# Attention scores: two heads turned in one block, and a high-by-high product of 64 rows

## The chip, the cores and the metric

The kernel runs on one core of one Trainium2 chip. The metric is the device time of one execution in microseconds (us); three runs of the kernel before gave a median of 2147.78 us, from 2147.52 to 2148.46. Engines are called as in the profile: PE (TensorE, matrix products and transposes; PEld is its loading of the stationary operand), DVE (VectorE), ACT (ScalarE), POOL (GpSimd) and SP (which issues the transfers).

## The reference

A trunk of two layers over 1024 tokens of width 1024. The first layer mixes tokens by a causal convolution, the second by attention in a sliding window of 128 keys with 16 query heads, 4 key and value heads (4 query heads share one) and head width 64. Each layer ends with layer norms, a squared-ReLU MLP of width 4096 and a gated embedding. All is float32. What the change touches is the scores of the attention:

```python
k = partial_rope((x @ w_k).reshape(B, T, N_KV_HEADS, HEAD_DIM), cos, sin)
q = partial_rope((x @ w_q).reshape(B, T, N_HEADS, HEAD_DIM), cos, sin)
q = q.reshape(B, nb, BLOCK, N_KV_HEADS, Q_PER_KV, HEAD_DIM)
scores = jnp.einsum("bnqkgd,bnskd->bnkgqs", q, kk,
                    preferred_element_type=jnp.float32) * (1.0 / math.sqrt(HEAD_DIM))
...
lse = jnp.logaddexp(jax.nn.logsumexp(scores, axis=-1, keepdims=True), sink)
probs = jnp.exp(scores - lse).astype(vv.dtype)
out = jnp.einsum("bnkgqs,bnskd->bnqkgd", probs, vv)
```

`kk` holds for each block of 128 queries the keys of the block before and of the own block; the first block has the own keys alone.

## The kernel before

**Two parts for each number.** A product in float32r (PE's faster format) keeps fewer bits than float32. So each operand is split into a high part, rounded to float32r, and a low part, the rest. `split` (line 652) does this with one ACT copy (high) and one DVE subtraction (low). `mm3` (line 656) then sums three products, high by high, high by low and low by high, in one PSUM bank.

**An order written by a planner.** The program is first recorded, each operation with an engine, its tiles and an assumed duration (`cost`, line 281). `schedule` (line 311) then plays the record through with these durations, gives tiles their buffers as they come free, and takes on each engine what is ready, the earliest recorded first. The engines run the result in that fixed order, so operations of neighbouring blocks stand mixed on each engine. All are issued from line 459, so the profile shows the same line everywhere, and groups are told apart by their tiles. Buffers are named by tag: `g` and `t` are tiles of 128x512 in SBUF, `B` holds keys (and later the residual stream), `ps`, `tr`, `sc`, `pv` are PSUM banks. `SLOTS` (line 47) says how many buffers each tag has; `move` hands a buffer from one tag to another. In the attention two `ps` banks become `sc`, one becomes `pv`.

**Keys** (in `attention`, line 1616). The projected keys and values of 8 token tiles come in two groups (tiles 4 to 7, then 0 to 3). For each tile, `rope` (line 1600) leaves 128 tokens x 4 heads x 64 in `kf`. It is split into high and low, the two laid side by side for each head in `kt`, and four transposes turn `kt`, one key head each: rows 0 to 63 of the result are the high part of the head, rows 64 to 127 the low part. Four ACT copies put them into `kT[g, half]`. For tiles 3 and 4 one more copy goes to `k34`, since block 4 needs keys of both halves of the tokens side by side.

**Queries and scores.** For each of 2 pairs of key heads and each of 8 blocks, 512 columns of queries (8 heads) are projected, and `rope` puts them into `q1`. POOL copies each head twice, side by side, into two tiles `qf`, one for each key head. `scores` (line 1729) is called once for each key head and block, 32 times in all. It turns its four heads with four transposes, so that rows 0 to 63 and rows 64 to 127 of the result both hold the head, and splits the result into `qT[0]` (high) and `qT[1]` (low). Each head then has two products of 128 rows with the same keys: `qT[0]` by `kT`, which gives high by high and high by low, and `qT[1]` by `kT`, which gives low by high and low by low:

```python
nc.tensor.matmul(ps[:, j, 0 : nb * P], qT[0][:, qs], ks, start=True, stop=False)
nc.tensor.matmul(ps[:, j, 0 : nb * P], qT[1][:, qs], ks, start=False, stop=True)
```

The scores have 256 columns (two blocks of keys), 128 in block 0. The rest of `scores` selects by mask (ACT copy, DVE `copy_predicated`), takes the maximum (DVE), the exponential with its sum (ACT) and the division (POOL). `values` (line 1780) runs two calls later: it turns the probabilities, splits them and multiplies by the values.

**Around it.** Before the attention stand the gated embedding of layer one, after it `mix_out` (output projection and layer norm). Both are long rows of PE products of 512 columns. The products of the query projections stand between those of the scores on PE.

Of the kernel before, what the change touches and what calls it, by code (L numbers as in the profile page):

```python
# [10 lines left out]
F32 = mybir.dt.float32  # L11
F32R = mybir.dt.float32r
AF = mybir.ActivationFunctionType
ALU = mybir.AluOpType

P = 128
# [7 lines left out]
HD = 64  # L24
# [7 lines left out]
WSLOTS = 5  # L32
# [7 lines left out]
LO = 288  # L40
LAG = 5
SC = 144
WAIT = 250.0
MIX_GROUPS = (
    ((0, 1, 2, 3), (4, 5, 6, 7)), ((0, 1), (2, 3), (4, 5), (6, 7)),
)
SLOTS = dict(raw=2, wh=WSLOTS, wl=WSLOTS, zz=1, A=9, B=8, X=8, E=4, bo=2, g=4, z=4, t=5, v=1, sm=16,
             ps=6, tr=2, sc=0, pv=0, mid=0)


# [139 lines left out]
class Recorder:  # L190
# [120 lines left out]
    def schedule(self):  # L311
# [85 lines left out]
        while True:  # L397
# [21 lines left out]
            p, i, o = heapq.heappop(rdy[e])  # L419
            if WAIT and fut[e] and e != "tensor":  # L420
                r, p2, i2, o2 = fut[e][0]
# [70 lines left out]
class Emit:  # L492
# [1123 lines left out]
    def attention(self):  # L1616
        nc, d, ws = self.nc, self.d, self.ws
        ac = self.sb("cst", n=256 + NT * 32 + 2 * NH)
        nc.sync.dma_start(ac[:, 0 : 256 + NT * 32], d["aconst"])
        self.own, self.ownT = ac[:, 0:P], ac[:, P : 2 * P]  # L1620
        self.rt = ac[:, 256 : 256 + NT * 32].rearrange("p (t e) -> p t e", t=NT)
        o = 256 + NT * 32
        self.sink, self.nsink = ac[:, o : o + NH], ac[:, o + NH : o + 2 * NH]
        nc.sync.dma_start(self.sink, d["sinks"].to_broadcast([P, NH]))
        nc.vector.tensor_scalar(out=self.nsink, in0=self.sink, scalar1=-1.0, scalar2=None, op0=ALU.mult)
        nc.vector.tensor_scalar(out=self.sink, in0=self.sink, scalar1=HD ** 0.5, scalar2=None, op0=ALU.mult)

        kT = {(g, p): self.sb("B", F32R) for p in range(2) for g in range(4)}  # L1630
        k34 = nc.tile("mid", (P, 1024), F32R).rearrange("p (g b t) -> p g b t", g=4, b=2)
        vf = [self.sb("A") for j in range(4)]
        ws.add(*[d["w_kv"][u] for u in range(4)])
        us = ws.get(4)
        for gp in range(2):
            ws.add(*self.low["w_q"][4 * gp : 4 * gp + 4])
        ws.pump()
        nc.move("raw", "mid")
        for tg in (range(4, 8), range(0, 4)):
            nc.slack = WORK_SLACK  # L1640
            for k in range(4 if tg[0] else 0):
                self.work("w_o", k, "X")
            nc.slack = 0.0
            for ps, t in zip(self.tok_group(tg, us), tg):
                nc.scalar.copy(vf[t // 2][:, t % 2 * 256 : (t % 2 + 1) * 256], ps[:, 256:512])
                kf = self.sb("t")[:, 0:256]
                self.rope(ps[:, 0:256], kf, t, 4)
                kt = self.sb("t", F32R)
                kv = kt.rearrange("p (g r e) -> p g r e", g=4, r=2)
                self.split(kf.rearrange("p (g e) -> p g e", g=4), kv[:, :, 0, :], kv[:, :, 1, :])  # L1650
                pt = self.transpose4(self.blocks(kt.bitcast(F32)))
                for g in range(4):
                    nc.scalar.copy(kT[g, t // 4][:, t % 4 * P : (t % 4 + 1) * P], pt[:, g * P : (g + 1) * P])
                if t in (3, 4):
                    nc.scalar.copy(k34[:, :, t - 3, :], pt.rearrange("p (g t) -> p g t", g=4))
        ws.done(4)
        self.kT, self.k34 = kT, k34

        for a, b in (("ps", "sc"), ("ps", "sc"), ("ps", "pv"), ("bo", "v"), ("bo", "v"), ("z", "v")):
            nc.move(a, b)  # L1660
        att = [self.pair("XE"[t // 4], F32R) for t in range(NT)]
        pend = []
        for gp in range(2):
            us = ws.get(4)
            for n in range(NT):
                ps = self.tok_group([n], us)[0]

                q1 = self.sb("t")
                self.rope(ps, q1, n, 8)
                qf = [self.sb("t") for gl in range(2)]  # L1670
                for gl in range(2):
                    src = q1[:, gl * 256 : (gl + 1) * 256].rearrange("p (h e) -> p h e", e=HD)
                    nc.gpsimd.tensor_copy(
                        qf[gl].rearrange("p (h r e) -> p h r e", r=2, e=HD), src.unsqueeze(2).to_broadcast([P, 4, 2, HD])
                    )

                col = n % 2 * 256 + gp * P
                own = vf[n // 2][:, col : col + P].rearrange("p (g e) -> p g e", g=2)
                if n == 0:
                    vd = [self.value_forms(own, q1 if gp == 0 else None)]  # L1680
                else:
                    if n > 1:
                        vd = [self.value_forms(last, q1 if n < 3 and gp == 0 else None)]
                    df = self.sb("t")[:, 0:P].rearrange("p (g e) -> p g e", g=2)
                    nc.vector.tensor_tensor(out=df, in0=own, in1=last, op=ALU.subtract)
                    vd = [vd[0], self.value_forms(df, q1 if n < 3 and gp == 0 else None)]
                last = own
                for gl in range(2):
                    if gp == 0:
                        dst = [a.rearrange("p (k t) -> p k t", k=4)[:, 2 * gl : 2 * gl + 2, :] for a in att[n]]  # L1690
                    else:
                        dst = [x[:, 2 * gl : 2 * gl + 2, n % 4 * P : (n % 4 + 1) * P] for x in self.xT[1, n // 4]]
                    p = self.scores(n, 2 * gp + gl, qf[gl])
                    pend.append((p, gl, vd, dst))
                    if len(pend) > 2:
                        self.values(*pend.pop(0))
            ws.done(4)
        for p in pend:
            self.values(*p)
        nc.move("mid", "raw")  # L1700
        for a, b in (("ps", "sc"), ("ps", "sc"), ("ps", "pv"), ("bo", "v"), ("bo", "v"), ("z", "v")):
            nc.move(b, a)

        self.x = []
        for t in range(NT):
            xt = [self.sb("AB"[t // 4]) for q in range(2)]
            for q in range(2):
                nc.sync.dma_start(xt[q], self.xsp[t // 4][t % 4 * P : (t % 4 + 1) * P, q * HT : (q + 1) * HT])
            self.x.append(xt)
        self.hid_tags = ("X", "E")  # L1710
        gb = self.load_row("g", d["mix_g"][1:2]), self.load_row("g", d["mix_b"][1:2])

        def lhs(t, kb):
            if kb < 4:
                return [a[:, kb * P : (kb + 1) * P] for a in att[t]]
            return self.xs(kb, t * P, P)

        self.mix_out(1, self.low["w_o"] + [d["w_o"][1, u] for u in range(4)], gb, range(NT), lhs)
# [10 lines left out]
    def scores(self, n, g, qf):  # L1729

        nc = self.nc
        nb = min(n, 1) + 1
        hs = slice(4 * g, 4 * g + 4)
        pq = self.transpose4(self.blocks(qf))
        qT = [self.sb("g", F32R) for j in range(2)]
        self.split(pq, *qT)
        sm = self.small(16)
        mx, nm, su = (sm[:, 4 * i : 4 * i + 4] for i in range(3))
        if n == 4:
            ks = self.k34[:, g].rearrange("p b t -> p (b t)")  # L1740
        else:
            o = (n % 4 + 1 - nb) * P
            ks = self.kT[g, n // 4][:, o : o + nb * P]

        s = nc.tile("z", (P, 4 * SC)).rearrange("p (h s) -> p h s", h=4)
        with nc.after(qf) if n == 0 else contextlib.nullcontext():
# [3 lines left out]
        for jj in range(2):  # L1750
            ps = self.ps("sc").rearrange("p (a b) -> p a b", a=2)
            for j in range(2):
                qs = slice((2 * jj + j) * P, (2 * jj + j + 1) * P)
                nc.tensor.matmul(ps[:, j, 0 : nb * P], qT[0][:, qs], ks, start=True, stop=False)
                nc.tensor.matmul(ps[:, j, 0 : nb * P], qT[1][:, qs], ks, start=False, stop=True)
            dst = s[:, 2 * jj : 2 * jj + 2, 0:P]
            if n:
                nc.scalar.copy(dst, ps[:, :, 0:P])
            nc.vector.copy_predicated(
                out=dst, mask=self.own.bitcast(mybir.dt.int32).unsqueeze(1).to_broadcast([P, 2, P]),  # L1760
                data=ps[:, :, (nb - 1) * P : nb * P],
            )
        nc.vector.reduce_max(out=mx, in_=s[:, :, 0:P], axis=mybir.AxisListType.X)
        nc.vector.scalar_tensor_tensor(
            out=nm, in0=mx, scalar=-(HD ** -0.5), in1=self.nsink[:, hs], op0=ALU.mult, op1=ALU.min
# [7 lines left out]
        for h in range(4):  # L1773
            nc.gpsimd.tensor_scalar(
                out=s[:, h, 0:P], in0=s[:, h, 0:P], scalar1=su[:, h : h + 1], scalar2=0.0,
# [170 lines left out]
```

## Time and profile before

| what | value |
|---|---|
| median of three runs | 2147.78 us |
| the profiled execution, its own time | 2149.95 us |
| its span in the profile | 2148.2 us |
| queries, scores and values (first to last product of scores) | 1175.6 to 1350.6 us |
| keys and values projected and turned | 1135 to 1175.6 us |

A row of the profile's groups gives line, engine, operation, tiles (result <- sources, buffer numbers left out), shapes and count, then the busy time, the mean duration of one, and the time the engine idled before them. A matmul row ends with the columns of its result: 128x512 is a product of 512 columns, and 128*128 says that its stationary operand has 128 rows and 128 columns. A transpose is a matmul with the tile `ident` among its operands. Products overlap on PE: each has a duration of its own, and what it costs in a dense row is the distance from its start to the next start. A row of the timeline gives the start, the time up to the last end, and how many like instructions stand in it.

### The profile page before, as it was taken

Reading aid. Unit: us, or ns where it says so; the run is one execution under the profiler, and the core shown is the slowest. Engines: PE = TensorE matmul, PEld = TensorE weight load, DVE = VectorE, ACT = ScalarE, POOL = GpSimd, SP = SyncE. Lnnn points to the kernel's source line nnn. Section 1 sums busy time; section 2 is a strip of 40 time slices with the busy share of each in tenths; the row PEclk is TensorE's granted clock in tenths of the full one; section 3 lists DMA queues with packets and bytes.
Section 4 is the critical chain, followed back from the end, with each engine's and each line's share of the span. In section 5 each row is a group of like instructions: output and inputs, shape, how many; then the busy total and the mean of one; then the engine's idle time right before and its main releaser. Section 6 shows DMA issues by size and latency. Waiting matters only on the chain.

```text
span 2148.2 us, 29826 instructions
## 1 busy us (share of the span) xinstructions
PE 2130.2 (99%) x10084; PEld 1765.3 (82%) x10084; DVE 1756.9 (82%) x2821; ACT 1096.2 (51%) x2098; POOL 285.5 (13%) x510
## 2 busy tenths in 40 slices
PE   9999999999999999999999999999999999999999
PEld 7888888888888888888788878887888888888877
DVE  6667788999897788876984888689999888788688
ACT  5333353655554533335855888455455454333484
POOL 0000052200000000001320656240000000000042
PEclk9999999999999999999999999999999999999999
DMA  7443554878786755655487022765788785575726
GB/s 237 114 111 89 171 178 172 263 233 272 257 268 223 281 174 197 204 186 216 150 283 254 11 89 70 228 227 182 252 288 294 272 300 169 182 235 169 262 75 230
DMA packets 203113, 433.21 MB, mean 202 GB/s; under 512 B 22353, under 2 KB 50641, under 8 KB 202961
## 3 DMA queue, kind: packets, MB, share of 16 engines
q1 hardware_dynamic: 202960, 431.32, 60.8%
q8 instruction: 79, 1.29, 0.2%
q14 instruction: 74, 0.60, 0.1%
HBM read 286.79 MB, written 144.44 MB: 201 GB/s over the span
## 4 chain that ended last, share of the span: by engine, by line
PE 45%; ACT 2%; DVE 2%; DMA 2%; issue 1%; POOL 0%; POOLq 0%; ACTq 0%; DVEq 0%
PE ps L459 34%; PE tr L459 11%; ACT z L459 1%; DVE z L459 0%; DVE B L459 0%; DMA raw<-form 0%; DMA wl<-gate_low_t 0%; DMA xh<-in_w_gate_dram 0%; POOL sm L459 0%; ACT xh L459 0%; DMA raw<-gate_t 0%; ACT t L459 0%; DVE t L459 0%; DMA raw<-in_w_q_dram 0%; ACT wh L459 0%
## 5 line engine op out<-in xcount | busy, mean ns | idle before, releaser
L459 PE MATMUL ps<-xh 128*128 128x512 f32 x618 | 240.4, 389 | 0.0
L459 PE MATMUL ps<-xl,xh 128*128 128x512 f32 x618 | 240.4, 389 | 0.0
L459 PE MATMUL ps<-xh,xl 128*128 128x512 f32 x618 | 240.4, 389 | 0.0
L459 PE MATMUL ps<-xh,wh 128*128 128x512 f32 x588 | 229.3, 394 | 0.9 <-ACT xh L459 0.9
L459 PE MATMUL ps<-xl,wh 128*128 128x512 f32 x588 | 229.4, 391 | 0.2 <-DVE xl L459 0.2
L459 PE MATMUL ps<-xh,wl 128*128 128x512 f32 x588 | 228.8, 390 | 0.0
L459 ACT CAST wh<-raw 128x1024 fp32r<-128x1024 f32 (+2 forms) x156 | 145.6, 937 | 128.4 <-PE ps L459 72.0
L459 POOL TENSOR_SCALAR sm<-sm 128x1 f32<-128x1 f32 x72 | 26.6, 373 | 1366.2 <-DVE E L459 612.8
L459 PE MATMUL ps<-wh,xh 128*128 128x512 f32 (+1 forms) x492 | 195.6, 398 | 2.5 <-DVE t L459 1.5
L459 PE MATMUL ps<-wl,xh 128*128 128x512 f32 (+1 forms) x492 | 195.5, 397 | 0.6 <-DMA wl<-gate_low_t 0.6
L459 PE MATMUL ps<-wh,xl 128*128 128x512 f32 (+1 forms) x492 | 195.6, 398 | 0.0
L459 ACT CAST wh<-g 128x512 fp32r<-128x512 f32 x108 | 64.5, 620 | 153.6 <-PE ps L459 75.3
L459 ACT CAST xh<-wh 128x1024 fp32r<-128x1024 f32 x76 | 79.7, 1049 | 118.3 <-PE ps L459 90.9
L459 PEld LDWEIGHTS ps<-xh 128*128 128x128 f32 x618 | 116.0, 188 | 24.2
L459 PEld LDWEIGHTS ps<-xh,xl 128*128 128x128 f32 x618 | 116.0, 188 | 24.1
L459 PEld LDWEIGHTS ps<-xl,xh 128*128 128x128 f32 x618 | 116.0, 188 | 24.0
L459 PEld LDWEIGHTS ps<-xh,wh 128*128 128x128 f32 x588 | 110.8, 188 | 25.6 <-ACT xh L459 1.3
L459 PEld LDWEIGHTS ps<-xh,wl 128*128 128x128 f32 x588 | 110.4, 188 | 23.4
L459 PEld LDWEIGHTS ps<-xl,wh 128*128 128x128 f32 x588 | 110.7, 188 | 21.8 <-DVE xl L459 0.7
L459 DVE TENSOR_TENSOR wl<-raw,wh 128x1024 fp32r<-128x1024 f32 (+1 forms) x100 | 101.2, 1013 | 25.3 <-ACT wh L459 24.5
L459 DVE TENSOR_TENSOR E<-cst,g 128x1152 fp32r<-128x1152 f32 x64 | 86.1, 1353 | 43.1 <-PE ps L459 40.9
L459 DVE TENSOR_TENSOR xl<-wh,xh 128x1024 fp32r<-128x1024 f32 x76 | 92.8, 1221 | 29.1 <-ACT xh L459 29.1
(441 smaller groups left out, 5402.5 us busy)
## 6 DMA issues: line engine op xcount, KB each, us to landing
wh<-hid SPq DMA_DIRECT2D x78, 512.0 KB, 4.1
raw<-in_w_up_dram SPq DMA_DIRECT2D x61, 512.0 KB, 4.3
wl<-in_w_down_dram SPq DMA_DIRECT2D x58, 512.0 KB, 4.8
hid<-zz SPq DMA_DIRECT2D x96, 256.0 KB, 4.2
hid<-t SPq DMA_DIRECT2D x70, 256.0 KB, 2.9
raw<-hid SPq DMA_DIRECT2D x30, 512.0 KB, 3.8
scr<-zz SPq DMA_DIRECT2D x128, 64.0 KB, 2.1
B<-scr SPq DMA_DIRECT2D x32, 256.0 KB, 4.1
```

What stands on the lines that cost most here:

```text
L459: getattr(getattr(nc, o.eng), o.name)(*a, **k)
```

## The change

Keys: `kf`, not its split parts, is turned, two heads in one transpose, two transposes a tile. Head g then stands in rows 0 to 63 (even g) or 64 to 127 (odd g): its `own` rows. ACT copies the high part to new tiles `kH`; DVE subtracts it from PSUM into the own rows of `kT`, which so holds the low part there, and ACT copies the high part into the other rows. `kH` takes two buffers each from `g` and `t` until the last block.

Queries: the copies on POOL go. `scores` turns two heads in one transpose, two transposes a call. Head 2j+e of the call stands in rows e*64 and on, columns j*128 and on. The split takes two ACT copies and two DVE subtractions of 64x256, which put the high part into the own rows of one tile `qT` and the low part into the other rows. One product of 128 rows then gives high by low and low by high (crosswise), and one product of 64 rows, own rows alone, high by high. Low by low is no longer formed. Block 4, whose high keys stand in two tiles, has two products of 64 rows and 128 columns in place of one of 256. The heads of the two banks are numbered so that order and results stay the same.

The core of the diff:

```diff
+ROWS = slice(0, P // 2), slice(P // 2, P)
+KH_FROM = "ggtt"
...
+        kH = {(j, p): self.sb("kh", F32R) for p in range(2) for j in range(2)}
...
+        for a in KH_FROM:
+            nc.move(a, "kh")
...
-                kt = self.sb("t", F32R)
-                kv = kt.rearrange("p (g r e) -> p g r e", g=4, r=2)
-                self.split(kf.rearrange("p (g e) -> p g e", g=4), kv[:, :, 0, :], kv[:, :, 1, :])
-                pt = self.transpose4(self.blocks(kt.bitcast(F32)))
+                pt = self.transpose4([kf[:, j * P : (j + 1) * P] for j in range(2)])
+                cols = slice(t % 4 * P, (t % 4 + 1) * P)
+                for j in range(2):
+                    nc.scalar.copy(kH[j, t // 4][:, cols], pt[:, j * P : (j + 1) * P])
                 for g in range(4):
-                    nc.scalar.copy(kT[g, t // 4][:, t % 4 * P : (t % 4 + 1) * P], pt[:, g * P : (g + 1) * P])
-                if t in (3, 4):
-                    nc.scalar.copy(k34[:, :, t - 3, :], pt.rearrange("p (g t) -> p g t", g=4))
+                    own, other = ROWS[g % 2], ROWS[1 - g % 2]
+                    hi = kH[g // 2, t // 4][own, cols].bitcast(F32)
+                    dst = kT[g, t // 4]
+                    nc.vector.tensor_tensor(
+                        out=dst[own, cols], in0=pt[own, g // 2 * P : (g // 2 + 1) * P], in1=hi, op=ALU.subtract
+                    )
+                    nc.scalar.copy(dst[other, cols], hi)
+                    if t in (3, 4):
+                        nc.scalar.copy(k34[:, g, t - 3, :], dst[:, cols].bitcast(F32))
...
-                qf = [self.sb("t") for gl in range(2)]
-                for gl in range(2):
-                    src = q1[:, gl * 256 : (gl + 1) * 256].rearrange("p (h e) -> p h e", e=HD)
-                    nc.gpsimd.tensor_copy(
-                        qf[gl].rearrange("p (h r e) -> p h r e", r=2, e=HD), src.unsqueeze(2).to_broadcast([P, 4, 2, HD])
-                    )
...
+        for a in KH_FROM:
+            nc.move("kh", a)
...
-        pq = self.transpose4(self.blocks(qf))
-        qT = [self.sb("g", F32R) for j in range(2)]
-        self.split(pq, *qT)
+        pq = self.transpose4([qf[:, j * P : (j + 1) * P] for j in range(2)])
+        own, other = ROWS[g % 2], ROWS[1 - g % 2]
+        qT = self.sb("g", F32R)
+        src = [(qT[own, e * 256 : (e + 1) * 256], qT[other, e * 256 : (e + 1) * 256], pq[ROWS[e], 0:256]) for e in range(2)]
+        for hi, lo, ps in src:
+            nc.scalar.copy(hi, ps)
+        for hi, lo, ps in src:
+            nc.vector.tensor_tensor(out=lo, in0=ps, in1=hi.bitcast(F32), op=ALU.subtract)
...
         if n == 4:
             ks = self.k34[:, g].rearrange("p b t -> p (b t)")
+            kh = [(0, P, self.kH[g // 2, 0][own, 3 * P :]), (P, P, self.kH[g // 2, 1][own, 0:P])]
         else:
             o = (n % 4 + 1 - nb) * P
             ks = self.kT[g, n // 4][:, o : o + nb * P]
+            kh = [(0, nb * P, self.kH[g // 2, n // 4][own, o : o + nb * P])]
...
-                qs = slice((2 * jj + j) * P, (2 * jj + j + 1) * P)
-                nc.tensor.matmul(ps[:, j, 0 : nb * P], qT[0][:, qs], ks, start=True, stop=False)
-                nc.tensor.matmul(ps[:, j, 0 : nb * P], qT[1][:, qs], ks, start=False, stop=True)
+                qs = slice((jj + 2 * j) * P, (jj + 2 * j + 1) * P)
+                nc.tensor.matmul(ps[:, j, 0 : nb * P], qT[:, qs], ks, start=True, stop=False)
+                for o, w, k in kh:
+                    nc.tensor.matmul(ps[:, j, o : o + w], qT[own, qs], k, start=False, stop=o + w == nb * P)
```

More of the change, by code (lines that the diff above doesn't have):

```diff
@@ L46 @@
 )
-SLOTS = dict(raw=2, wh=WSLOTS, wl=WSLOTS, zz=1, A=9, B=8, X=8, E=4, bo=2, g=4, z=4, t=5, v=1, sm=16,
+SLOTS = dict(raw=2, wh=WSLOTS, wl=WSLOTS, zz=1, A=9, B=8, X=8, E=4, bo=2, g=4, z=4, t=5, v=1, kh=0, sm=16,
              ps=6, tr=2, sc=0, pv=0, mid=0)
@@ L1647, in attention @@
                 self.rope(ps[:, 0:256], kf, t, 4)
-                kt = self.sb("t", F32R)
-                kv = kt.rearrange("p (g r e) -> p g r e", g=4, r=2)
-                self.split(kf.rearrange("p (g e) -> p g e", g=4), kv[:, :, 0, :], kv[:, :, 1, :])
-                pt = self.transpose4(self.blocks(kt.bitcast(F32)))
+                pt = self.transpose4([kf[:, j * P : (j + 1) * P] for j in range(2)])
+                cols = slice(t % 4 * P, (t % 4 + 1) * P)
+                for j in range(2):
+                    nc.scalar.copy(kH[j, t // 4][:, cols], pt[:, j * P : (j + 1) * P])
                 for g in range(4):
-                    nc.scalar.copy(kT[g, t // 4][:, t % 4 * P : (t % 4 + 1) * P], pt[:, g * P : (g + 1) * P])
-                if t in (3, 4):
-                    nc.scalar.copy(k34[:, :, t - 3, :], pt.rearrange("p (g t) -> p g t", g=4))
+                    own, other = ROWS[g % 2], ROWS[1 - g % 2]
[7 more added lines that the diff above has]
+                        nc.scalar.copy(k34[:, g, t - 3, :], dst[:, cols].bitcast(F32))
         ws.done(4)
-        self.kT, self.k34 = kT, k34
+        self.kT, self.k34, self.kH = kT, k34, kH
         for a, b in (("ps", "sc"), ("ps", "sc"), ("ps", "pv"), ("bo", "v"), ("bo", "v"), ("z", "v")):
@@ L1692, in attention @@
                         dst = [x[:, 2 * gl : 2 * gl + 2, n % 4 * P : (n % 4 + 1) * P] for x in self.xT[1, n // 4]]
-                    p = self.scores(n, 2 * gp + gl, qf[gl])
+                    p = self.scores(n, 2 * gp + gl, q1[:, gl * 256 : (gl + 1) * 256])
                     pend.append((p, gl, vd, dst))
```

## The prediction

> **What bounds the kernel now.** I read the page first, then the busy time by stretches around the attention, then the groups by shape inside it, the waits of PE, and last the timeline of PE, where the cost of single products can be read.
>
> ```profile
> span 2148.2 us, 29826 instructions
> PE 2130.2 (99%) x10084; PEld 1765.3 (82%) x10084; DVE 1756.9 (82%) x2821; ACT 1096.2 (51%) x2098; POOL 285.5 (13%) x510
> PEclk9999999999999999999999999999999999999999
> PE 45%; ACT 2%; DVE 2%; DMA 2%; issue 1%; POOL 0%; POOLq 0%; ACTq 0%; DVEq 0%
> ```
>
> PE is busy for 99% of the span, at full granted clock in every slice, and leads the chain that ended last. A product taken away there should be time saved, as long as its place is dense. So I looked at the stretches that the change touches (keys; queries, scores and values; the output projection):
>
> ```profile
> core 0: us, PE busy (x) PEld busy (x) DVE busy (x) ACT busy (x) POOL busy (x), PEclk, DMA share, GB/s
> 1135.00:1175.60 40.60, 40.23 (x198) 33.23 (x197) 18.12 (x60) 26.98 (x81) 2.50 (x7) 1.00 0.81 277
> 1175.60:1350.60 175.00, 174.09 (x985) 143.59 (x984) 151.14 (x403) 147.90 (x493) 106.49 (x260) 1.00 0.20 64
> 1350.60:1400.00 49.40, 49.40 (x223) 40.22 (x222) 29.44 (x52) 18.69 (x44) 5.73 (x12) 1.00 0.72 233
> ```
>
> In the 175 us of the scores PE is busy for 174.1, but DVE has 151.1 (86%) and ACT 147.9 (85%) as well: the other engines have some 24 us of room, no more. The view of the waits names for PE from 1190 to 1352 us only two, of 0.3 and 0.2 us:
>
> ```profile
> PE ps L459 <- POOL z L459: 0.3, 1, 0.3
> PE tr L459 <- DVE t L459: 0.2, 1, 0.2
> ```
>
> Busy time hides short pauses, since products overlap, so the cost of one product has to be read from starts. The timeline of PE in the scores:
>
> ```profile
> 1202.00 0.40 PE L459 MATMUL ps<-wl,xh 128*128 128x512 f32 x1
> 1202.23 0.39 PE L459 MATMUL ps<-wh,xl 128*128 128x512 f32 x1
> 1202.46 0.60 PE L459 MATMUL ps<-ident,t 128*128 128x128 f32 x4
> ...
> 1222.78 0.64 PE L459 MATMUL ps<-raw,g 128*128 128x256 f32 x4
> 1223.26 0.39 PE L459 MATMUL ps<-wh,xl 128*128 128x512 f32 x1
> ...
> 1225.32 0.39 PE L459 MATMUL ps<-wh,xl 128*128 128x512 f32 x1
> 1225.78 0.47 PE L459 MATMUL ps<-A,v 128*128 128x512 f32 x1
> ```
>
> A product of 512 columns is followed by the next start after 0.23 us. Four products of 256 columns take 1223.26 - 1222.78 = 0.48 us from start to start, 0.120 each. Four transposes end 0.60 us after the first start; one lasts 0.272 us by its row below, so their starts are (0.60 - 0.272) / 3 = 0.109 us apart. The last two rows show a pause that no view calls idle: 0.46 us in place of 0.23.
>
> ```profile
> L459 PE MATMUL tr<-B,g x112: 221/282/389, 1175.8 to 1349.4; 128*128 128x256 f32 x96, 128*128 128x128 f32 x16
> L459 PE MATMUL ps<-ident,t x132: 270/272/276, 1139.7 to 1343.4; 128*128 128x128 f32 x132
> L459 PE MATMUL ps<-wh,xl x195: 388/393/481, 1135.2 to 1399.5; 128*128 128x512 f32 x195
> ```
>
> **The change, part by part.** *Transposes.* The 32 calls of `scores` have two fewer each, the 8 key tiles two fewer each: 64 + 16 = 80. At 0.109 us that is -8.7 us of PE in dense stretches.
>
> *Products of the scores.* Each head keeps two products, one now with 64 rows. Block 4 has three: 4 key heads x 4 heads = 16 products of 256 columns become 32 of 128 columns. At the cost of a transpose for 128 columns, 32 x 0.109 - 16 x 0.120 = +1.6 us. The balance of PE, if 64 rows cost what 128 do, is -7.1 us. It also counts as 80 - 16 = 64 fewer instructions, 10020 in place of 10084, which the program of the changed kernel has.
>
> *Products of 64 rows among those of 128.* Every product of the profile before is 128*128, so no row shows what a change of the row count costs. In the order that the planner writes for the changed kernel there are 144 products of 64 rows, mostly single (the crosswise product of a head, then its high-by-high product): PE goes from one row count to the other 252 times. Bounds: the end on the one side is nothing. Changes of another kind, from product to transpose and back, stand in the rows above at no cost (0.109 and 0.23 us are the same there as in rows of a kind), and this is the row that speaks for nothing. The end on the other side is the part of a product that the next one overlaps: a product of 256 columns lasts 0.282 us and the next starts after 0.120, so 0.162 us would be exposed if a product of another row count had to wait until the one ahead has left the array. It is the same 0.16 us for 512 columns (0.39 - 0.23) and for a transpose (0.272 - 0.109). That is 252 x 0.162 = 40.8 us. A change of kind keeps the 128x128 shape, so its rows do not settle what another row count does, and no pair of products in the trace differs in it. I can exclude neither end and take the middle, 0.08 us, an estimate from the two: +20.2 us. Break-even is at 7.1 / 252 = 0.028 us, so five sixths of the way between the ends lie on the slower side.
>
> The Trainium skill speaks against the change here: in its page TensorEngine Tiling (Array Packing), section Key Properties, "Mode switching requires drain". It gives no price; by it the case of no cost would be out, and nothing in this case's trace can yet show whether that is so.
>
> Could products of 64 rows be cheaper than those of 128? The distances above go with columns (0.23, 0.120, 0.109), and at 128 columns something other than columns holds them. Loading is the candidate:
>
> ```profile
> L459 PEld LDWEIGHTS tr<-B,g 128*128 128x128 f32 x96 | 15.1, 189 | 4.5 <-ACT g L459 1.7 <-DVE g L459 0.8 <-DVE z L459 0.5
> L459 PEld LDWEIGHTS ps<-ident,t 128*128 128x128 f32 x96 | 12.1, 140 | 2.9
> ```
>
> A shorter load (140 against 189 ns) does not make transposes closer than 0.109 us, so I expect no gain from fewer rows; the end of the range for it is 96 products of 256 columns at 0.109 in place of 0.120, about -1 us.
>
> *The split.* DVE, ACT and POOL rows of the scores:
>
> ```profile
> L459 DVE TENSOR_TENSOR g<-ps,g 128x512 fp32r<-128x512 f32 x27 | 18.5, 690 | 4.0 <-ACT g L459 3.7
> L459 DVE TENSOR_TENSOR t<-t,ps 64x256 f32<-64x256 f32 x58 | 24.6, 424 | 6.6 <-ACT t L459 4.4
> L459 ACT CAST g<-ps 128x512 fp32r<-128x512 f32 x27 | 15.6, 581 | 1.0 <-PE ps L459 0.7
> L459 ACT COPY t<-ps 64x256 f32<-64x256 f32 x58 | 21.0, 362 | 6.7 <-PE ps L459 3.9 <-DVE t L459 2.1
> L459 POOL COPY t<-t 128x512 f32<-128x512 f32 x30 | 18.5, 630 | 19.5 <-DVE t L459 7.1 <-issue 6.0 <-ACT z L459 3.5
> ```
>
> One subtraction of 128x512 (0.690) becomes two of 64x256 (0.424 each, the row of the same shape): +0.158 us x 32 = +5.1 us of DVE. One copy of 0.581 becomes two of 0.362: +0.143 x 32 = +4.6 us of ACT. Against the room of 24 us this is hidden behind PE: DVE would have 156 of some 168 us. 32 copies of 0.63 us leave POOL, and with them a step of 0.6 to 1.3 us between rope and the transposes, so the queries are ready earlier. I cost all this at nothing; without that cover it costs at most what is added, 9.7 us.
>
> *Keys.* In each tile the split of `kf` (one ACT copy, one DVE subtraction) and four ACT copies become two ACT copies, four subtractions and four copies of 64x128; tiles 3 and 4 have four copies of 128x128 in place of one of 128x512.
>
> ```profile
> L459 ACT CAST B<-ps 128x128 fp32r<-128x128 f32 x24 | 5.7, 292 | 1.4 <-PE ps L459 1.2
> L459 DVE TENSOR_TENSOR t<-t,t 128x256 fp32r<-128x256 f32 x8 | 3.4, 424 | 3.4 <-ACT t L459 3.3
> L459 DVE TENSOR_TENSOR zz<-ps,cst 128x32 f32<-128x32 f32 x14 | 2.3, 182 | 0.0
> ```
>
> With no subtraction of 64x128 in the trace I bound it by the two DVE rows, 0.182 and 0.424 us: 4 x 0.182 - 0.424 = +0.3 to 4 x 0.424 - 0.424 = +1.3 us a tile on DVE, two more ACT copies of 0.29 us less the one of `kt`. DVE is at 18 of 40.6 us in this stretch and ACT at 27, and the long rows of products around it cover it. The last tile of keys is followed by the projection of the first queries on PE, so nothing there is late by more than the chain's one more step, under 1 us.
>
> *Buffers.* `kH` leaves `g` two buffers and `t` three while the scores run. `qT` needs one `g` per call in place of two, and `qf` no `t` at all in place of two per block, so neither has less for its use than before. SP's queue issues the same loads in nearly the same order; none waits for a tile of the change but the two pairs of `g` rows for the layer norm after the attention, which are used tens of us later.
>
> **The sum.** -8.7 + 1.6 + 20.2 = +13.1 us. The profiled execution took 2149.95 us (span 2148.2 and 1.75 us around it), 2.2 us above the median of 2147.78; 2149.95 + 13.1 = 2163.0, and against the median 2147.8 + 13.1 = **2160.9 us**.
>
> **The rivals.** *No cost of a change of rows (not slower).* Then PE alone decides: -7.1 us, 2140.6. For it speaks that changes between products and transposes cost nothing, and that 64 products of 0.11 us go from dense stretches; against it, that it is one end of a wide interval, and that a change of kind is not one of rows. It holds as long as a change costs under 0.028 us. Where the pauses as after 1225.32 swallow part of the gain it ends up to 4 us higher.
>
> *The whole overlap is exposed.* 252 x 0.162 - 7.1 = +33.7 us: 2181.5. For it speaks that the three shapes have the same 0.16 us; against it, that it is the other end, and that no change in the trace exposes any of it.
>
> *DVE and ACT take over.* Were their added 9.7 us all on the path, with a free change of rows: -7.1 + 9.7 = +2.6 us, 2150.4. Against it stand 24 us of room; for it, that both are at 85% and the order is fixed. *The change does not do what it says*: the transposes go, but PE waits in their place for the same chain of mask, maximum and exponential. This gives 2147.8; the waits of PE (0.3 and 0.2 us) speak against it.
>
> **How the numbers follow.** Forecast (a change costs 0.045 to 0.13 us, 2152 to 2173): 0.40. Whole overlap and beyond: 0.15. No cost: 0.37. The last two rivals, and a change near break-even: 0.08. A measurement of this kernel can tell about 0.2%, 4.3 us, from no change. Slower by more than that is forecast and whole overlap, 0.55; faster 0.37; within 0.08. The range reaches from the no-cost case (2140.6, with 1 us for cheaper loads and 1.6 for fewer pauses) to the whole overlap: 2138 to 2182. The forecast's own range is 2152 to 2173.
>
> **What would show it.** In the profile after, 10020 matmuls; groups `ps<-B,g` and `tr<-B,g` of 128 rows and new ones of 64 rows. In the timeline, a crosswise product followed by its 64-row product after 0.12 us means no cost, after 0.20 the forecast, after 0.28 the whole overlap; likewise the start after a 64-row product. The stretch of the scores should grow from 175 us to about 188 (167 without cost), while the rest of the span keeps its length. DVE's two subtractions per call should show 0.42 us each and the POOL copies be gone. The prediction is wrong if the 64-row products follow at 0.12 us, or if the time moves outside this stretch.

## The result and the profile after

The changed kernel takes 2186.19 us (median of four runs, 2183.6 to 2188.6); the kernel before takes 2147.89 beside it. The ratio is 1.0178, 95% interval 1.016 to 1.0195: slower by 38.3 us. Forecast were 2160.9 and a range up to 2182, so the time lies 4.2 us above the range. Two of the four runs had a granted clock of 1.000 over the whole span and took 2183.6 and 2184.1 us, the other two had 0.998 and took 2188.3 and 2188.6.

The page of after: span, engines, and the chain that ended last by engine.

```profile
span 2181.9 us, 29736 instructions
PE 2165.4 (99%) x10020; PEld 1771.7 (81%) x10020; DVE 1770.9 (81%) x2877; ACT 1110.9 (51%) x2144; POOL 266.8 (12%) x478
PEclk9999999999999999999999999999999999999999
PE 44%; ACT 2%; DVE 2%; DMA 2%; issue 1%; POOL 0%; DVEq 0%; SPq 0%; ACTq 0%; POOLq 0%
```

PE has 64 products fewer and is busy 35 us longer, at the same clock. Busy time by stretches (the same columns as in the prediction) shows where:

```profile
1135.00:1175.60 40.60, 39.90 (x184) 31.82 (x182) 24.41 (x86) 32.24 (x96) 0.00 (x0) 1.00 0.76 263
1175.60:1390.00 214.40, 213.17 (x951) 153.31 (x950) 159.78 (x436) 159.31 (x535) 90.80 (x233) 1.00 0.18 58
1390.00:1440.00 50.00, 50.00 (x223) 41.20 (x223) 32.88 (x56) 17.82 (x34) 6.03 (x14) 1.00 0.71 225
```

The first product of the scores starts at 1173.9 us, the last at 1383.3: 209 us in place of 175. What lies before and after keeps its length within 2 us. PE is nearly always busy there, and DVE and ACT have a smaller share than before (about 75% in place of 85 to 86%): the products themselves take longer. The timeline of PE and of its loading (PEld), two heads of one call:

```profile
1237.02 0.40 PE L461 MATMUL ps<-wh,xl 128*128 128x512 f32 x1
1237.17 0.19 PEld L461 LDWEIGHTS tr<-B,g 128*128 128x128 f32 x1 [0.18 <-issue]
1237.26 0.29 PE L461 MATMUL tr<-B,g 128*128 128x256 f32 x1
1237.48 0.18 PEld L461 LDWEIGHTS tr<-t,g 64*128 64x128 f32 x1
1237.48 0.38 PE L461 MATMUL tr<-t,g 64*128 64x256 f32 x1
1237.79 0.19 PEld L461 LDWEIGHTS ps<-B,g 128*128 128x128 f32 x1
1237.79 0.39 PE L461 MATMUL ps<-B,g 128*128 128x256 f32 x1
1238.10 0.18 PEld L461 LDWEIGHTS ps<-t,g 64*128 64x128 f32 x1
1238.11 0.38 PE L461 MATMUL ps<-t,g 64*128 64x256 f32 x1
1238.42 0.19 PEld L461 LDWEIGHTS ps<-wh,xh 128*128 128x128 f32 x1
1238.42 0.50 PE L461 MATMUL ps<-wh,xh 128*128 128x512 f32 x1
```

The same views of before, in a dense row of products:

```profile
1223.49 0.40 PE L459 MATMUL ps<-wh,xh 128*128 128x512 f32 x1
1223.49 0.19 PEld L459 LDWEIGHTS ps<-wl,xh 128*128 128x128 f32 x1
1223.73 0.39 PE L459 MATMUL ps<-wl,xh 128*128 128x512 f32 x1
```

Before, the operand of the next product is loaded while the present one runs: the load stands at the start of the product ahead. After, at each of the 252 changes of the row count, the load stands at the start of its own product, within 4 ns. Two things are lost there. The next start comes late: 0.22 us after the first 128-row product (1237.26 to 1237.48; the median of such pairs is 0.21) in place of 0.12. And the load is then on the path: the product lasts 0.38 in place of 0.28, so that its own successor starts 0.31 us later (1237.48 to 1237.79). Over all pairs of the scores in the trace the median distance is 311 ns from a 64-row product of 256 columns, itself just behind a change, to a 128-row one, where 119 is usual; so a change costs 0.19 us, 0.09 for the late start and 0.10 for the bare load.

### The profile page after: what moved, and what is told of

Its sections match the earlier page's. It is cut to its first block, busy times and chain, and to the rows that moved or that the text cites. A ratio compares the mean times of both kernels' runs of the same rounds, so it can differ in the third digit from the quotient of the medians.

```text
span 2181.9 us, 29736 instructions
## 1 busy us (share of the span) xinstructions
PE 2165.4 (99%) x10020; PEld 1771.7 (81%) x10020; DVE 1770.9 (81%) x2877; ACT 1110.9 (51%) x2144; POOL 266.8 (12%) x478
## 4 chain that ended last, share of the span: by engine, by line
PE 44%; ACT 2%; DVE 2%; DMA 2%; issue 1%; POOL 0%; DVEq 0%; SPq 0%; ACTq 0%; POOLq 0%
PE ps L461 33%; PE tr L461 11%; ACT z L461 1%; DMA hid<-zz 1%; DMA raw<-in_w_up_dram 1%; DVE wl L461 0%; DVE t L461 0%; DVE g L461 0%; POOL sm L461 0%; DVE zz L461 0%; ACT xh L461 0%; DMA raw<-gate_t 0%; ACT t L461 0%; DMA gate_low_b<-xl 0%; DVE xl L461 0%
## 5 line engine op out<-in xcount | busy, mean ns | idle before, releaser
L461 ACT CAST wh<-g 128x512 fp32r<-128x512 f32 x95 | 57.8, 621 | 153.8 <-PE ps L461 80.2
```

The lines of the kernel that those rows point to most:

```text
L461: getattr(getattr(nc, o.eng), o.name)(*a, **k)
```

## The experiments

Theory 1 is this price of a change. Its rivals were that 64-row products are dear in themselves (2) and that split, keys or buffers hold PE up (3). Four runs tell them apart.

**Undo the row count alone (e1).** The extra term (low query by the other head's high keys) is told in the expectation.

```diff
...
-kh = [(0, nb * P, self.kH[g // 2, n // 4][own, o : o + nb * P])]
+kh = [(0, nb * P, self.kH[g // 2, n // 4][:, o : o + nb * P])]
...
-nc.tensor.matmul(ps[:, j, o : o + w], qT[own, qs], k, ...)
+nc.tensor.matmul(ps[:, j, o : o + w], qT[:, qs], k, ...)
```

> The changed kernel, its high-by-high product with all 128 rows of the same two tiles (it then also adds the low part of the query by the high keys of the other head, so the scores differ slightly). Order, transposes, split and buffers stay as in the changed kernel; only the row count goes. Theory 1 (each change of PE between 64 and 128 rows costs about (38.3 + 7.1) / 252 = 0.18 us): no changes left, 2147.9 - 7.1 = 2140.8 us. Theory 2 (a 64-row product itself is dear, 45.4 / 144 = 0.315 us each, whatever stands beside it): the same 2140.8. Theory 3 (the split on DVE and ACT, the keys or the buffers hold PE up): it stays near 2186.

Measured: 2154.2 us, ratio 1.0028 (1.0018 to 1.0038). 32.0 of the 38.3 us go with the row count; the traces of the two kernels have the same order on PE, DVE, ACT and POOL. But the kernel stays 13.4 us above PE's sum of 2140.8, and is slower than before even without 64-row products.

**The row count alone, in the kernel before (e2).**

```diff
-nc.tensor.matmul(ps[:, j, 0 : nb * P], qT[1][:, qs], ks, start=False, stop=True)
+nc.tensor.matmul(ps[:, j, 0 : nb * P], qT[1][0:HD, qs], ks[0:HD], start=False, stop=True)
```

> The kernel before, its second product of each head (low queries) with rows 0 to 63 alone, which leaves out low by low. Nothing else changes; 128 products of 64 rows, 224 changes of the row count in the order. Theory 1: 2147.9 + 224 x 0.18 = 2188 us. Theory 2: 2147.9 + 128 x 0.315 = 2188. Theory 3: 2148, since split, transposes and buffers are those of before.

Measured: 2185.2 us, 1.0173 (1.0157 to 1.0188): +37.3 for 224 changes, 0.166 each. The row count does it with the split, the transposes, the buffers and the order of before. (Theory 2 expects the same here; e3 and e4 separate it.)

**Fewer changes, the same products (e3)** (the loop over `j` is run once for the crosswise and once for the high products).

> The changed kernel with the two heads of a bank in the order crosswise, crosswise, high, high: 132 changes of the row count in place of 252, the same 144 products of 64 rows. Theory 1: 2140.8 + 132 x 0.18 = 2164.6 us; up to 8 more if a 64-row product right after another one costs 0.05 to 0.1 more, as a few pairs in the changed kernel's trace do (163 ns where 109 is usual). Theory 2: 2186, the count of 64-row products is the same. Theory 3: about 2186.

Measured: 2162.5 us, 1.0068 (1.0053 to 1.0083). That is 2 us below theory 1's 2164.6. Theory 2 is out: as many 64-row products cost 23.7 us less.

**More 64-row products, fewer changes (e4)** (the edit of e2 on both products).

> The kernel before with both products of each head on rows 0 to 63 alone (it leaves out high by low and low by low): 256 products of 64 rows, but only 136 changes of the row count, 188 places where one 64-row product follows another. Theory 1: 2147.9 + 136 x 0.18 = 2172 us, and 9 to 19 more if the second of two 64-row products costs 0.05 to 0.1 more. Theory 2: 2147.9 + 256 x 0.315 = 2229. Theory 3: 2148.

Measured: 2167.5 us, 1.009 (1.0075 to 1.0105): +19.6 for 136 changes, 0.144 each. Theory 2 is out by 61 us. The timeline shows a run of four 64-row products:

```profile
1241.07 0.73 PE L459 MATMUL ps<-B,g 64*128 64x256 f32 x4
1241.73 0.66 PE L459 MATMUL tr<-ident,t 128*128 128x128 f32 x4
```

From 1241.07 to 1241.73 there are four starts with two changes at their ends; inside such runs the median distance is 118 ns, as with 128 rows (119). Rows cost nothing, changing them does.

*Why 128 rows throughout does not reach 2140.8.* Three reasons were put to the test: the split (A), the buffers (B) and the planner's durations (C).

**High by high through zeros (e5)**: `qZ` (own rows zero, other rows the high part) times `kT`, in place of `qT[own]` times `kH`; `kH` goes.

> No product of 64 rows and no high-key tiles: high by high multiplies the keys' tile itself (low part in the own rows, high part in the other rows) by a second query tile that holds zero in the own rows and the high part in the other rows (zeros set once, the high part copied by POOL). Two transposes a call, the split in 64x256 pieces and the planner's durations stay; all five t buffers are back, g serves two calls at a time as in the changed kernel; block 4 needs no third product. PE alone: 80 transposes less, 2147.9 - 8.7 = 2139.2 us. The kernel with 128 rows throughout lost 13.4 us against its own sum (2154.2 against 2140.8). Theory A (the split's added DVE and ACT time makes PE wait): about 2152. Theory B (the buffers taken from t and g): about 2140. Theory C (the planner's durations for the 64x256 pieces are too short, so the order on the engines is wrong): about 2152.

Measured: 2157.1 us, 1.0038 (1.0026 to 1.0051). Theory B finds no support: with all five `t` buffers back the kernel is not faster. Two buffers of `g` still go to `qZ`, though, and each call has one more copy on POOL ahead of its second product, which could hide a gain.

**The split in halves, in the kernel before (e6).**

```diff
-self.split(pq, *qT)
+cs = [slice(e * 256, (e + 1) * 256) for e in range(2)]
+for c in cs: nc.scalar.copy(qT[0][:, c], pq[:, c])
+for c in cs: nc.vector.tensor_tensor(out=qT[1][:, c], in0=pq[:, c], in1=qT[0][:, c].bitcast(F32), op=ALU.subtract)
```

> The kernel before with the split of the queries in two column halves of 128x256: two ACT copies of some 0.37 us and two DVE subtractions of some 0.43 in each call, as much as the changed kernel's 64x256 pieces take; everything else as before. Theory A: 2147.9 + about 10 = 2158 us. Theory B: 2148. Theory C: about 2158, since the planner assumes the same short durations here.

Measured: 2148.8 us, 1.0 (0.9991 to 1.0009). In the kernel before, the pieces cost nothing. Whether they do where PE has less to do was not tested.

**The planner's durations (e7, e8)** (85 ns more for the 64-row pieces of `g`), on e1 and e5.

> The changed kernel with 128 rows throughout (high by high adds the low part of the query by the other head's high keys), and with 85 ns more assumed by the planner for each 64-row copy and subtraction of the query split: 362 and 424 ns, as measured for that shape, in place of 278 and 337. Only the order on the engines can change. Theory A: 2154, as without. Theory B: 2154. Theory C: 2141 to 2146.

> The kernel with zero rows and, as in the one before this, the longer durations assumed by the planner. Theory A: about 2152 us. Theory B: about 2140, as without them. Theory C: 2139 to 2144, and below the kernel with zero rows by some 8.

Measured: 2156.8 and 2160.8 us, 2.6 and 3.7 above the same kernels without, with intervals that overlap, where theory C needs at least 8 below. Theory C falls. (Over the scores of e8 the granted clock was 0.97, and 1.00 in e5, so part of the 3.7 us may be the clock's.) Against A and C speaks e6; but none of the three was found to account for 13 us. So I looked at who leads. The chain of waits inside the scores, shares by engine and tile, for before, for 128 rows throughout, and for after:

```profile
by line: PE ps L459 75.8%; PE tr L459 12.3%; DMA raw<-in_w_q_dram 2.9%; ACT z L459 2.6%; issue 0.8%; ACT wh L459 0.8%; DVE A L459 0.8%; DVE t L459 0.7%; DVE sm L459 0.7%; DVE z L459 0.7%; ACT t L459 0.5%; DVE g L459 0.4%; ACT g L459 0.3%; A
```

```profile
by line: PE ps L461 32.9%; ACT z L461 12.3%; PE tr L461 6.3%; ACT t L461 5.6%; DVE t L461 5.3%; ACT g L461 4.9%; DVE g L461 4.8%; DVE z L461 4.7%; DVE sm L461 4.1%; issue 3.3%; DMA raw<-in_w_q_dram 2.3%; ACT wh L461 2.3%; DVE A L461 2.2%; A
```

```profile
by line: PE ps L461 78.3%; PE tr L461 17.6%; ACT z L461 1.2%; ACT t L461 0.9%; ACT g L461 0.5%; issue 0.5%; DVE t L461 0.4%; ACT A L461 0.3%; DVE g L461 0.2%; ACT xh L461 0.1%; ACT v L461 0.1%
```

Before, PE has 88% of the chain; in after 96%. With 128 rows throughout it has 39%, and most of the rest are single pieces of ACT and DVE. So theory D: with fewer transposes the scores are no longer set by PE, and work taken from it comes back as waits.

**Leave PE's work out (e12).**

> The changed kernel with the 144 high-by-high products left out (the scores lack them, so the output is another): 15 us of PE work less than in the first experiment, the same split, chain and maximum. Theory D: PE does not set the length of the scores any more, so most of it comes back as waits: 2148 to 2154 us. If PE still sets it: 2139.

Measured: 2151.8 us, 1.0016 (1.0006 to 1.0026): 144 products fewer give 2.4 us, 15 had PE set the time. That is theory D's number. In this profile the granted clock fell too, by 3% over the stretch:

```profile
1174.00:1352.00 178.00, 165.59 (x790) 123.16 (x789) 153.92 (x424) 153.61 (x517) 87.70 (x226) 0.97 0.21 66
```

The traces part the two. As waits of PE I count, from the first to the last product of the scores, what each distance between starts has above the usual one (0.109, 0.120 and 0.230 us for 128, 256 and 512 columns; above 0.03 us). Before has 13.6 us of them, e1 24.0 and e12 38.6. Of e12's, 5.3 lie in three stretches of 3.4 us in which the granted clock was 0.5. So some 9 of the 15 us came back as waits at full clock, and 5 went with the clock.

**Leave DVE's work out (e9, e10, e11)** (the exponential subtracts the sink in place of the maximum), with 128 rows, in before, and in after:

```diff
-nc.vector.reduce_max(out=mx, in_=s[:, :, 0:P], axis=mybir.AxisListType.X)
-nc.vector.scalar_tensor_tensor(out=nm, in0=mx, scalar=-(HD ** -0.5), in1=self.nsink[:, hs], op0=ALU.mult, op1=ALU.min)
+nm = self.nsink[:, hs]
```

> The changed kernel with 128 rows throughout (as in the first experiment) and without the maximum of the scores: the exponential subtracts the sink instead, which leaves the quotient the same; 32 reductions of 0.68 us and 32 small operations leave DVE, and two steps leave the chain between mask and exponential. Theory D (DVE and ACT, busy for 153 of 178 us in the scores, and the chain through both keep PE waiting, so PE work taken away there comes back as waits): the waits of 19 us shrink, 2141 to 2146 us against 2154.2. Theory E (PE waits for something else, as the loss has nothing to do with DVE): 2154.

> The kernel before without the maximum of the scores, the control. PE has 167 us of work in the scores and 8 us of waits. Theory D: 2140 to 2146, at most the 8 us less. Theory E: 2148. The distance to the changed kernel with 128 rows and without the maximum is then what two transposes a call are worth on PE: by theory D some -5 to -7 us, as the sum of the prediction had it.

> The changed kernel, with its 64-row products, without the maximum. By theory D waits on PE hide part of the price of the 252 changes of the row count; with fewer waits the price is seen whole: 0.18 to 0.19 us each, 45 to 48 us above the same kernel with 128 rows, where 32 us (0.127 each) were seen with the maximum; about 2188. If the price of a change is 0.127 us whatever hides it: 32 us above.

Measured: 2148.7 (1.0005, 0.9996 to 1.0014), 2147.1 (0.9998, 0.9988 to 1.0007) and 2183.5 us (1.0166, 1.0151 to 1.0181). With 128 rows 5.5 us come back (the waits fall from 24.0 to 19.8), in before 0.9, and in after 2.7. That is theory D's direction, but short of its 2141 to 2146, and in before the 2147.1 is nearer to theory E's 2148; the two transposes a call are still worth nothing (2148.7 against 2147.1). The price of the changes is 34.8 us here, 0.138 each, not the 45 to 48 that theory D expects but close to the 32 of its rival: that waits hide part of the price is not shown by this pair.

**Relieve ACT as well (e13 to e16).** POOL copies the high parts of the attention's output and of the values:

```diff
+    def pool_split(self, src, h, l):
+        self.nc.gpsimd.tensor_copy(h, src)
+        self.nc.vector.tensor_tensor(out=l, in0=src, in1=h.bitcast(F32), op=ALU.subtract)
...
-        self.split(src, v[:, :, 1, :], v[:, :, 0, :])
+        self.pool_split(src, v[:, :, 1, :], v[:, :, 0, :])
...
-        self.split(o, *dst)
+        self.pool_split(o, *dst)
```

> The changed kernel with 128 rows throughout, without the maximum, and with the high parts of the attention's output and of the values copied by POOL in place of ACT (about 32 x 0.40 and 29 x 0.29 us). Theory F (DVE and ACT together set the length of the scores): with both relieved the waits of PE fall towards those of before, 2141 to 2144 us. Theory G (something else, such as the PSUM banks or the tiles for probabilities, paces the calls): 2148.7, as without POOL's help.

> The same with the maximum kept, so that only ACT is relieved. Theory F: between 2141 and 2154, about 2148, as DVE's relief alone gave 2148.7. Theory G: 2154.

> The control: the kernel before without the maximum and with POOL's copies. PE's own work sets it, with 8 us of waits: theory F 2143 to 2147 us, and 4 to 7 us above the kernel with two transposes a call. Theory G: 2147.

> The kernel with zero rows in a second query tile (exact high by high with 128 rows), without the maximum and with POOL's copies. PE's sum is 1.6 us less than in the first of these. Theory F: 2139 to 2145 us, below before. Theory G: about 2151 (2157 less the 5.5 of the maximum).

Measured: 2147.9 (0.9997, 0.9989 to 1.0006), 2151.2 (1.0016, 1.0007 to 1.0025), 2146.7 (0.9995, 0.9986 to 1.0004) and 2148.5 us (1.0007, 0.9998 to 1.0015). The relief of ACT alone gives 3 us, on top of DVE's about 1 (2148.7 to 2147.9, within the noise): theory F has the direction and half of the size at most, and its 2141 to 2144 are not reached; e15 lies where both theories put it. In e13 the chain has PE in front again, with ACT's work on `z` (the scores) and the loads of the query weights next, which have 2.9% of the chain of before too:

```profile
by line: PE ps L461 61.6%; PE tr L461 12.0%; ACT z L461 6.1%; DMA raw<-in_w_q_dram 3.4%; DVE g L461 2.7%; ACT t L461 2.4%; ACT g L461 2.1%; issue 1.8%; ACT wh L461 1.7%; DVE A L461 1.6%; DVE z L461 1.3%; DVE xl L461 1.0%; DVE t L461 1.0%; A
```

One such load makes ACT wait for 2.08 us, then DVE, then a product of the scores:

```profile
1240.64 1.04 ACT L461 CAST wh<-raw 128x1024 fp32r<-128x1024 f32 x1 [2.08 <-DMA raw<-in_w_q_dram]
1241.71 0.37 ACT L461 COPY z<-tr 128x256 f32<-128x256 f32 x1
...
1242.11 0.44 DVE L461 COPY_PREDICATED z<-cst,tr 128x256 f32<-128x256 int32 x1 [2.25 <-ACT z L461]
...
1242.61 0.38 PE L461 MATMUL tr<-B,g 128*128 128x256 f32 x1 [1.79 <-DVE z L461]
```

**Plan the products of the scores later (e17, e18)** (`nc.slack = 600.0` around them), since the added waits stood before them.

> The changed kernel with 128 rows throughout, split and maximum as they are, and the products of the scores planned 0.6 us later behind the subtraction that they wait for (a slack in the planner; only the order changes). Theory H (the planner puts these products just behind their last piece, and on the chip PE comes to them too early, 67 times, each time some 0.15 us): the waits before them fall from 9.9 us to 2 to 4, and the time from 2154.2 to 2146 to 2149. Theory G (the calls are paced by something else): the waits move to other products and the time stays at 2152 to 2156.

> The kernel with zero rows, no maximum and POOL's copies, its score products planned 0.6 us later in the same way: the best of all that was tried, exact in its products. Its waits before scores are 4.2 us, before values 7.3. Theory H: about 2 us less than the 2148.5 without the slack, 2145 to 2147, just below before. Theory G: 2148.5.

Measured: 2154.3 (1.0035, 1.0023 to 1.0047) and 2146.9 us (0.9996, 0.9988 to 1.0005). In the first, by the same count as above, waits before scores fell from 10.9 to 7.1 us (the expectation's count gave 9.9), and those before values rose from 4.7 to 6.5 and before transposes from 3.2 to 5.2; the sum stayed at 24.0. They moved, as theory G has it, and theory H falls here, also because its 2 to 4 us were not reached. The second lies at theory H's number, 1.6 us below e16, but the intervals of the two overlap, so it decides nothing. It is the fastest form of the change; its interval takes in no difference, so nothing that was tried beats the kernel before.

## Why the prediction was wrong, point by point

**Transposes and products of the scores (-8.7 and +1.6).** The counts hold: 10020 matmuls. The time is not to be had: with 128 rows throughout the kernel is 6.3 us slower than before, not 7.1 faster. (16 of the 80 transposes lie in the stretch of the keys, so by the prediction's own sum the scores would have taken 190 us, 170 without cost, not 188 and 167; they took 209.)

**Products of 64 rows among those of 128.** This step failed, in its term of +20.2 us: "I can exclude neither end and take the middle, 0.08 us". The count of 252 changes and the direction hold, the price does not. A change costs 0.19 us in the trace, 48 us in all. In time the row count is worth 32.0 us by e1 (0.13 a change) and 34.8 by e11 (0.14); e2 gives 37.3 / 224 = 0.17 and e4 19.6 / 136 = 0.14. Against e1, which ACT and DVE hold up, e3 gives only 8.3 / 132 = 0.06. In e3's own chain PE has 96%, and counted from PE's sum of 2140.8 it gives 0.16, and after 45.4 / 252 = 0.18.

What the term left out is the load. 0.162 was no upper end: it held the overlap of two products, but not that the next operand is loaded under the product ahead. That load, 0.18 us in PEld, starts only with its own product at each change, and 0.10 us of it lies bare. The late start alone, 0.09 us, is close to the middle of 0.08, and the start after a crosswise product, 0.21, to the 0.20 named for the forecast; but no row stood behind the middle, so that is luck. The start after a 64-row product, 0.31, is beyond the 0.28 named for the whole overlap. Rows of before showed that there was a load ahead to lose; that a change of rows loses it they could not show. The rule of the Trainium skill that a change of tiling mode drains the engine (TensorEngine Tiling (Array Packing), Key Properties) names neither a price nor the late load. By the trace the next start does come late, 0.21 us in place of 0.12, but still ahead of the end that the profile gives the product before it (0.28).

**Fewer rows give no gain.** Right: 118 ns inside runs of 64 rows, 119 with 128.

**The split, at nothing.** Wrong as a reason, hidden in the result. DVE and ACT at 85% do not leave 24 us of room: in e1, where PE has some 7 us less to do, PE has only 39% of the chain, and the kernel stands 13.4 us above PE's sum. In after, where PE has 96% of the chain, the slow products cover them again; the sum of PE alone, 2140.8 + 252 x 0.19 = 2188.7, comes near the measured 2186.2. The pieces themselves cost nothing in e6; that the shorter row on PE lays the chain bare is what e12 and e9 speak for. That the fixed orders are the reason is argued, not shown.

**Rivals.** "The whole overlap is exposed" (2181.5) came nearest, 4.7 us short, but by luck: of the 0.162 us some 0.09 are exposed, and the load gives the rest. "DVE and ACT take over" (2150.4) and the rival that PE waits for the same chain in place of the transposes (2147.8) did not set the time of after. They tell what happens with 128 rows (2154.2), the second better than the first, since the added pieces cost nothing in e6; neither has the size.

**Keys, buffers, the rest of the span.** The keys and the rest are right: the first product of the scores starts 1.9 us earlier (1173.9 in place of 1175.8), and what lies behind the scores keeps its length within 1 us. The buffers of `t` come back in e5 without a gain; those of `g` came back in no run, so for them it stays open.

**Open.** With DVE and ACT both relieved and two transposes a call the kernel stands at 2147.9, not at 2141. PE's waits in the scores are 19.4 us there, 13.6 in before. Its trace shows the loads of the query weights and many short waits in turn; which of them paces the calls was not settled.

## What to carry to other kernels

Products of fewer rows are as cheap as full ones only among their own kind: count how often the order changes the row count, and price each change with the loss of the load that runs ahead, not with the overlap of two products alone. Before counting a saving on an engine that is 99% busy, look whether another chain has nearly the same length; two engines at 85% that wait for each other were not 15% of room here. A cheap test is to leave work of the leading engine out: when 15 us fewer give 2.4, it does not lead. Look at the granted clock of that run as well.

## What the runs showed of the hardware that was not expected

A product of 128 rows after one of 64, or the other way round, does not have its operand loaded ahead: in after the load starts within 4 ns of its own product at all 252 changes (also at the 224 of e2 and the 136 of e4), while between products of like rows it starts with the product ahead (in before, median 3 ns behind that one's start). Of 64-row products of 256 columns in a row (e4), the first after a change is followed after 223 ns, the later ones after 118.

The granted clock, 1.00 over the scores in before and in after, fell to 0.5 within the scores in three stretches of 3.4 us in the profile of e12 and in stretches of 6.8 and 3.4 us in that of e8, 0.97 on average in both. These are the two profiles with the most waits on PE in the scores of those counted (38.6 and 32.0 us); e5 with 28.5 has 1.00. What sets the clock off was not tested.
